# A feed-forward block's first stage: one width tile in full products in place of two, the next two in step, and four places for the last rows' inputs

## The chip, the cores and the metric

The kernel runs on one core of a Trainium2 chip. A core has a matmul engine (TensorE, in the profile PE, with its weight loads PEld), a vector engine (VectorE, DVE), an activation engine (ScalarE, ACT), a general engine (GpSimd, POOL) and a queue engine that issues most transfers (SyncE, SP). Each works through its own instructions in order; semaphores let one wait for another. Data lie in HBM, are brought into the on-chip SBUF by DMA, and matmuls write PSUM, which is in banks of 128 x 512 float32.

The metric is the device time of one execution in microseconds, as the median of several runs.

## What is computed

The reference is an encoder of two layers over 1024 tokens of width 1024. The token mixer is windowed attention in layer 0 and a gated linear recurrence in layer 1. Both layers end with the same kind of feed-forward block (ConvGLU), and it is this block that the change touches:

```python
def conv_ffn(v, w_in, conv_w, conv_b, w_out):
    gate, up = jnp.split(v @ w_in, 2, axis=-1)
    hid = jax.nn.gelu(dwconv_centred(gate, conv_w, conv_b)) * up
    return hid @ w_out

# of each layer, behind the mixer:
    f = conv_ffn(rmsnorm(h, norm_g[layer, 2]), ffn_w_in[layer], ffn_conv_w[layer],
                 ffn_conv_b[layer], ffn_w_out[layer])
    h = h + rmsnorm(f, norm_g[layer, 3])
```

`w_in` is 1024 x 5632, `w_out` 2816 x 1024, all in float32. The depthwise convolution runs along the tokens and is three wide.

## The kernel before

**Precision.** Every float32 operand of a matmul is split into a high part (a cast on ACT, line 88) and a low part (the difference, on DVE, line 89); a product is three matmuls, high by high, high by low and low by high (`mmk`, lines 531 to 538). Group names such as `wl<-st,wh` or `u7l<-c,u7h` are these low parts: `w` of weights, `u` of the activations. `uh` and `ul` hold the normalised activations of the block, transposed: 8 tiles of 128 of the width (k) by 1024 tokens. `ti` and `tj` are the two halves of the tokens, in layer 1 in the other order.

**The first stage** (`ffn`, from line 541; `first_units`, lines 680 to 741) makes gate and up for 22 tiles of 128 of the hidden width, one tile f after the other. A tile can be made in two ways:

- *In full* (`plain`, line 576): four PSUM groups, gate and up by ti and tj, each of 8 k-tiles by 3 matmuls, 96 matmuls of 128 x 512. It needs `uh` and `ul` as they are and two weight units made by `wunit`.
- *By block products* (`prod`, line 650): a Strassen-like scheme with seven products in place of eight, each of 4 k-tiles by 3 matmuls, so 84 matmuls. Product k multiplies a part of a weight unit (`operand`, line 645) with an operand B[k] made of the activations. B1, B2 and B3 are parts of `uh` and `ul` themselves; B4, B6 and B7 are made on DVE and ACT in tiles of their own, and B5 is written over the part of `uh` and `ul` with k 0 to 3 and tokens tj, so it can only be made when nobody needs that part any more. `operands` (line 597) makes them, in two halves of 128 x 1024 each.

The weight units of a tile in block products are four: a1 straight from HBM, the sums sx and sy, and a22. The sums are made by the DMA engines: `load` (line 622) issues plain loads of sx and sy on SP, and three accumulating transfers on POOL (line 632 into sx, lines 633 and 634 into the two halves of sy, each behind the one before it). a1 serves products 1 and 2, sx 5 and 7, sy 6 and 3, a22 product 4. `weights` (line 636) splits them into a ring of four places.

Before the change tiles 0 and 1 are made in full (`PLAIN = 2`). While PE works on them, DVE and ACT make the operands; after tile 1's full products B5 is split over its place. Tiles 2 to 21 follow in block products, in the order 2, 5, 6, 7, 3, then product 1 of the next tile, then 4. Behind each tile, `conv` (line 564) applies convolution, gelu and gating on ACT and DVE, and `hidden` (line 662) stores halves and their combinations in HBM for the second stage.

**The second stage** (lines 744 to 868) multiplies the hidden values with `w_out`, also in block products: seven sweeps over the 11 pairs of width tiles, in the order 1, 6, 7, 4, 2, 5, 3. Each step loads its two operands into the staging pool (`st`, four places; lines 753 and 754), splits them, and runs on four PSUM groups. `tail` (line 793) finishes a block of 128 tokens: it loads the block of the residual (`x<-h1d`, line 796), sums two squared norms (798), takes the power -0.5 on POOL (95), scales and adds (802) and stores (806). In layer 0 (`gnext`) it also normalises and transposes for the next layer (`norm_T`, lines 107 to 118). The blocks of the first half are finished in the middle of sweep 5, those of the second half behind sweep 3. There, at lines 846 to 855, DVE adds the PSUM group to a stored part (`y1`, 852), ACT squares and sums it (102), DVE multiplies it in place with the norm's weights (854), and `tail` follows. `x` has two places, so the load for a block waits until the store of the one two before it is done.

**What sets the order.** The program is written as a sequence of operations on tiles; a scheduler of the framework sets each engine's order from a model of the costs, and waits are put where a place in a pool or an operand isn't free. So the order on an engine isn't that of the text: DVE, for instance, makes operands in between the splits of weights. SP issues loads and stores in one order, and a load that waits for its place holds the ones behind it.

Of the kernel before, what the change touches and what calls it, by code (L numbers as in the profile page):

```python
# [6 lines left out]
F32 = mybir.dt.float32  # L7
# [4 lines left out]
ALU = mybir.AluOpType  # L12
# [4 lines left out]
P = 128  # L17
T = 1024
# [24 lines left out]

PLAIN = 2
# [4 lines left out]
def build(tc, A, out):  # L49
# [490 lines left out]
    def ffn(l, wo, dst, gnext, halves_, out_halves):  # L540
# [35 lines left out]
        def plain(f):  # L576

            wg = wo.first if f == 0 and wo.first else wunit(A["ffw1"][l, f, :, :1024])
# [3 lines left out]
            for (wh, wl), ps, m in ((wg, gi, ti), (wu, ui, ti), (wg, gj, tj), (wu, uj, tj)):  # L582
                mmk(ps, KT, lambda k: (wh[:, k * P:(k + 1) * P], wl[:, k * P:(k + 1) * P]),
                    lambda k: (uh[:, k, m], ul[:, k, m]), True)
# [5 lines left out]
            return conv(f, g, u)  # L590

        def operands():

            b12 = (uh[:, :4, tj], ul[:, :4, tj])
            late = []
            for kk in range(2):
                ks = slice(2 * kk, 2 * kk + 2)
                f32 = lambda x: x[:, ks].bitcast(F32)
                def tmp(t, b=1):
                    return fp.tile([P, 2, 512], F32, tag=t, bufs=b, name=t)  # L600
                def both(o, x, y, sub):
                    q = tmp("tt", 2)
                    dve.tensor_tensor(o, f32(x[0]), f32(y[0]), op=ALU.subtract)
                    dve.tensor_tensor(q, f32(x[1]), f32(y[1]), op=ALU.subtract)
                    dve.tensor_tensor(o, o, q, op=ALU.add)
                def more(o, a_, x, op):
                    dve.tensor_tensor(o, a_, f32(x[0]), op=op)
                    dve.tensor_tensor(o, o, f32(x[1]), op=op)
                x = tmp("c", 3)
                both(x, B[3], b12, True)  # L610
                split(B[7][0][:, ks], B[7][1][:, ks], x)
                more(x, x, B[1], ALU.add)
                nsplit(B[6][0][:, ks], B[6][1][:, ks], x)
                more(x, x, B[2], ALU.subtract)
                split(B[4][0][:, ks], B[4][1][:, ks], x)
                e1 = tmp("u") if kk else tmp("g")
                both(e1, B[1], b12, True)
                late.append((ks, e1))
            return late
# [60 lines left out]
        def first_units():  # L680
            for f in range(PLAIN):
                c = plain(f)
                if f == 0:
                    late = operands()
# [613 lines left out]
```

## Time and profile before

| | |
|---|---|
| runs of the kernel | 2732.56, 2733.25 and 2733.93 us, median 2733.25 |
| the profiled execution | 2730.61 us, of which its span 2728.8 us |
| granted clock, mean over the span | 0.993 |
| first stage of layer 0, first matmul to the second stage's first | 595.29 to 1023.67 us |
| first stage of layer 1 | 2079.45 to 2509.02 us |

The profile shows one execution. Times in it are in microseconds from the start of the span, unless marked ns. A row of an engine's timeline gives start, duration, engine, line, operation and what is written from what (`out<-in`), its shape and how many instructions of the kind follow each other; in square brackets stands how long the engine was idle before it, and what it waited for. A row of waits gives the waiting engine and line, what it waited for, the sum, the times and the longest. The chain of waits follows the end of the program back to what released each step. Consecutive instructions overlap, so that the distance of two starts is a little shorter than a duration.

### The profile page before, as it was taken

What the parts mean: (1) busy time and instruction counts of PE and PEld (TensorE: products, weight loads), DVE (VectorE), ACT (ScalarE), POOL (GpSimd) and SP (SyncE); (2) the same over time, 40 slices, a digit from 0 to 9 for tenths busy, and PEclk for the clock granted to TensorE, in tenths of its full rate; (3) what the DMA queues carried; (4) which work ended last, traced back from release to release, by engine and by line L of the source; (5) the groups of instructions that cost most, each with busy time, mean ns of one, the idle gap of its engine ahead of it and who ended that gap; (6) DMA issues with size and microseconds to landing.
All of it is one profiled execution on the core that took longest, in us unless ns stands there. A gap on an engine that the chain in (4) does not pass through costs nothing.

```text
span 2728.8 us, 37469 instructions
## 1 busy us (share of the span) xinstructions
PE 2660.9 (98%) x13496; PEld 2231.2 (82%) x13496; DVE 1828.1 (67%) x3034; ACT 1391.6 (51%) x2550; POOL 463.3 (17%) x514
## 2 busy tenths in 40 slices
PE   8999999999999999999999999999899999999998
PEld 7888887788888888887888888888788788888886
DVE  6588787678555565477686777868566856556446
ACT  6367667544444445454444545545454444444443
POOL 1231110211111100032232231312121111110013
PEclk9999999999999999999999999999999999999999
DMA  8683213656777857673234531111476687775666
GB/s 282 208 176 86 63 51 97 200 187 151 202 200 189 210 152 236 200 248 131 86 124 119 117 86 55 46 55 33 125 221 174 155 208 203 202 200 157 225 193 228
DMA packets 213579, 428.45 MB, mean 157 GB/s; under 512 B 20368, under 2 KB 77072, under 8 KB 207760
## 3 DMA queue, kind: packets, MB, share of 16 engines
q1 hardware_dynamic: 187264, 333.50, 38.0%
q0 software_dynamic: 23680, 88.09, 15.7%
q10 hardware_dynamic: 2448, 4.46, 0.5%
q8 instruction: 106, 1.74, 0.3%
q14 instruction: 81, 0.66, 0.1%
HBM read 333.17 MB, written 117.96 MB: 165 GB/s over the span
## 4 chain that ended last, share of the span: by engine, by line
PE 88%; DVE 7%; ACT 2%; DMA 1%; issue 1%; POOL 1%; SPq 0%; DVEq 0%; POOLq 0%; ACTq 0%
PE X L537 28%; PE V L537 11%; PE pj L83 7%; PE pj L84 7%; PE pj L85 7%; PE Y L537 5%; PE pb L83 3%; PE pb L84 3%; PE pb L85 3%; PE po L1118 1%; PE pa L1070 1%; PE pt L340 1%; PE pt L118 1%; PE pa L1050 1%; PE pu L1094 1%
## 5 line engine op out<-in xcount | busy, mean ns | idle before, releaser
L89 DVE TENSOR_TENSOR wl<-st,wh 128x1024 fp32r<-128x1024 f32 (+1 forms) x234 | 258.7, 1110 | 337.9 <-ACT wh L88 330.6
L88 ACT CAST wh<-st 128x1024 fp32r<-128x1024 f32 (+1 forms) x234 | 219.1, 938 | 291.3 <-PE X L537 180.9
L83 PE MATMUL pj<-uh,wh 128*128 128x512 f32 x512 | 206.3, 403 | 6.4 <-DVE xl L89 4.6
L537 PE MATMUL X<-wl,wh 128*128 128x512 f32 x528 | 205.7, 391 | 0.0
L537 PE MATMUL X<-wh,wl 128*128 128x512 f32 x528 | 205.5, 391 | 0.0
L84 PE MATMUL pj<-ul,wh 128*128 128x512 f32 x512 | 203.0, 397 | 0.1
L537 PE MATMUL X<-wh 128*128 128x512 f32 x528 | 201.0, 392 | 1.9 <-DVE c L846 1.9
L85 PE MATMUL pj<-uh,wl 128*128 128x512 f32 x512 | 202.9, 397 | 0.0
L83 PE MATMUL pj<-wh,uh 128*128 128x384 f32 (+1 forms) x512 | 190.8, 373 | 0.4 <-DVE v L282 0.4
L84 PE MATMUL pj<-wl,uh 128*128 128x384 f32 (+1 forms) x512 | 186.9, 365 | 0.0
L85 PE MATMUL pj<-wh,ul 128*128 128x384 f32 (+1 forms) x512 | 186.7, 365 | 0.0
L79 DVE TENSOR_TENSOR wl<-st,wh 128x1024 fp32r<-128x1024 f32 (+1 forms) x96 | 118.9, 1245 | 27.0 <-ACT wh L78 26.0
L537 PE MATMUL V<-uh,wh 128*128 128x512 f32 x344 | 133.9, 389 | 0.3 <-ACT uh L88 0.3
L537 PE MATMUL V<-ul,wh 128*128 128x512 f32 x344 | 134.0, 389 | 0.0
L537 PE MATMUL V<-uh,wl 128*128 128x512 f32 x344 | 133.9, 389 | 0.0
L78 ACT CAST wh<-st 128x1024 fp32r<-128x1024 f32 (+1 forms) x103 | 103.9, 1016 | 48.7 <-PE pj L84 27.2
L83 PEld LDWEIGHTS pj<-uh,wh 128*128 128x128 f32 x512 | 97.1, 190 | 26.7 <-DVE xl L89 5.5
L537 PEld LDWEIGHTS X<-wh 128*128 128x128 f32 x528 | 99.4, 188 | 23.8 <-issue 2.7
L1064 POOL TENSOR_TENSOR E<-EP,q 128x256 f32<-128x256 f32 x64 | 54.4, 850 | 371.3 <-DVE EP L1057 292.6
L537 PEld LDWEIGHTS X<-wl,wh 128*128 128x128 f32 x528 | 99.5, 189 | 21.0 <-DVE wl L89 0.5
L537 PEld LDWEIGHTS X<-wh,wl 128*128 128x128 f32 x528 | 99.5, 189 | 21.0
L85 PEld LDWEIGHTS pj<-uh,wl 128*128 128x128 f32 x512 | 97.2, 190 | 19.6
(337 smaller groups left out, 7322.1 us busy)
## 6 DMA issues: line engine op xcount, KB each, us to landing
st<-hid SPq DMA_DIRECT2D x154, 256.0 KB, 3.2
st<-in_ffw_dram SPq DMA_DIRECT2D x106, 256.0 KB, 3.2
w2s<-in_ffw_dram POOLq DMA_DIRECT2D x24, 1024.0 KB, 8.0
st<-in_ffw_dram SPq DMA_DIRECT2D x48, 512.0 KB, 3.6
hid<-tt SPq DMA_DIRECT2D x88, 256.0 KB, 4.6
st<-w2s SPq DMA_DIRECT2D x88, 256.0 KB, 3.4
sx<-in_ffw_dram SPq DMA_DIRECT2D x80, 256.0 KB, 3.9
sy<-in_ffw_dram SPq DMA_DIRECT2D x40, 512.0 KB, 5.8
```

What stands on the lines that cost most here:

```text
L78: act.copy(h[:, :n], raw)
L79: (eng or dve).tensor_tensor(l[:, :n], raw, h[:, :n].bitcast(F32), op=ALU.subtract)
L83: pe.matmul(o, ah, bh, start=first, stop=False)
L84: pe.matmul(o, ah, bl, start=False, stop=False)
L85: pe.matmul(o, al, bh, start=False, stop=last)
L88: act.copy(h, src)
L89: dve.tensor_tensor(l, src, h.bitcast(F32), op=ALU.subtract)
L118: pe.transpose(ps[:, k, :], u[:, (4 * b + k) * P:(4 * b + k + 1) * P], ident)
L340: pe.transpose(tp[:, j, :], sm[:, j, c * P:(c + 1) * P], ident)
L537: pe.matmul(o, x, y, start=new, stop=e, skip_group_check=not first)
L1050: pe.matmul(pa[:, c, :], E2[:, cs], E1[:, cs], start=True, stop=True)
L1064: pool.tensor_tensor(gl, pl_, ql, op=ALU.mult)
```

## The change

In the first stage of both layers only tile 0 is made in full, and its two tj groups run k 0 to 3 first, then k 4 to 7. Tiles 1 and 2 are made in block products side by side, one product for both and then the next: 1 and 2 (which need only the activations of ti), 5, 3, 6, 7, 4. `operands` is now a generator that makes B5, then B6, B7 and B4, each from the one before by an addition or subtraction, and the program text calls it between the products. As a second tile is open, its up and gate values lie in places of the scratch pool `tt`, its product 5 in the place of `s1`. Tile 3's loads and splits begin during product 7, its products 2 and 1 (the first of the sequence from there) around product 4 of tiles 1 and 2. The store of the hidden values of tiles 0, 1 and 2 follows after that.

In the second stage, `rows` loads the residual's blocks ahead of `tail`. The four blocks of the second half are loaded together when the last sweep's matmuls are issued; in layer 0 they have four places in their own pool, in layer 1 they use the staging pool's. The product with the norm's weights goes to a tile of its own, `y2`, which no longer overwrites what ACT reads.

In the diff the body of the old `operands`, which the kernel's text above shows, is cut.

```diff
@@ -40,8 +40,6 @@
 
 LAST = (6, 10)
 HOLD = (4, 7)
-
-PLAIN = 2
 
 AHEAD = 2000
 
@@ -575,48 +573,61 @@
 
         def plain(f):
 
-            wg = wo.first if f == 0 and wo.first else wunit(A["ffw1"][l, f, :, :1024])
+            wg = wo.first if wo.first else wunit(A["ffw1"][l, f, :, :1024])
             wu = wunit(A["ffw1"][l, f, :, 1024:])
             bank = lambda t: psx.tile([P, 512], F32, tag=t, name=t)
             gi, ui, gj, uj = bank("X"), bank("Y"), bank("V"), bank("Y")
-            for (wh, wl), ps, m in ((wg, gi, ti), (wu, ui, ti), (wg, gj, tj), (wu, uj, tj)):
-                mmk(ps, KT, lambda k: (wh[:, k * P:(k + 1) * P], wl[:, k * P:(k + 1) * P]),
-                    lambda k: (uh[:, k, m], ul[:, k, m]), True)
+            def some(w, ps, ks, m, first):
+                wh, wl = w
+                mmk(ps, len(ks), lambda k: (wh[:, ks[k] * P:(ks[k] + 1) * P], wl[:, ks[k] * P:(ks[k] + 1) * P]),
+                    lambda k: (uh[:, ks[k], m], ul[:, ks[k], m]), first)
+            some(wg, gi, range(KT), ti, True)
+            some(wu, ui, range(KT), ti, True)
+
+            for ks in (range(4), range(4, KT)):
+                some(wg, gj, ks, tj, ks[0] == 0)
+                some(wu, uj, ks, tj, ks[0] == 0)
+            yield
             g = gtile()
             u = fp.tile([P, T], F32, tag="u", bufs=1, name="u")
             for gp, up_, m in ((gi, ui, ti), (gj, uj, tj)):
                 act.activation(g[:, m], gp, AF.Copy, scale=-1.0)
                 act.copy(u[:, m], up_)
-            return conv(f, g, u)
+            yield conv(f, g, u)
 
         def operands():
 
...
-            return late
+            xs = [fp.tile([P, 2, 512], F32, tag="c", bufs=3, name="c") for _ in range(2)]
+            tmp = lambda: fp.tile([P, 2, 512], F32, tag="tt", bufs=2, name="tt")
+            half = lambda x, kk: x[:, 2 * kk:2 * kk + 2]
+            def more(o, x, part, kk, op):
+                for c in range(2):
+                    dve.tensor_tensor(o, x, half(part[c], kk).bitcast(F32), op=op)
+                    x = o
+            def out_of(sp, k, kk, x):
+                sp(half(B[k][0], kk), half(B[k][1], kk), x)
+            for kk, x in enumerate(xs):
+                q = tmp()
+                f32 = lambda t, c: half(t[c], kk).bitcast(F32)
+                dve.tensor_tensor(x, f32(B[1], 0), f32(B[5], 0), op=ALU.subtract)
+                dve.tensor_tensor(q, f32(B[1], 1), f32(B[5], 1), op=ALU.subtract)
+                dve.tensor_tensor(x, x, q, op=ALU.add)
+            for kk, x in enumerate(xs):
+                out_of(split, 5, kk, x)
+            yield
+            for kk, x in enumerate(xs):
+                more(x, x, B[3], kk, ALU.add)
+                out_of(nsplit, 6, kk, x)
+            yield
+            for kk, x in enumerate(xs):
+                q = tmp()
+                more(q, x, B[1], kk, ALU.subtract)
+                out_of(split, 7, kk, q)
+            yield
+            for kk, x in enumerate(xs):
+                more(x, x, B[2], kk, ALU.subtract)
+                out_of(split, 4, kk, x)
+            yield
 
         def load(f):
 
@@ -678,29 +689,75 @@
                 nc.sync.dma_start(hd[k, p], x)
 
         def first_units():
-            for f in range(PLAIN):
-                c = plain(f)
-                if f == 0:
-                    late = operands()
-                hidden(f, c)
-                if f == PLAIN - 1:
-                    for ks, e1 in late:
-                        split(B[5][0][:, ks], B[5][1][:, ks], e1)
-            raws = {f: load(f) for f in (PLAIN, PLAIN + 1)}
-            gen = weights(raws.pop(PLAIN))
-            ops = list(gen)
-            X = [psx.tile([P, 512], F32, tag="X", name="X")]
-            s = {}
+            X, s, ops = [], {}, []
+
+            def xbank():
+                X.append(psx.tile([P, 512], F32, tag="X", name="X"))
 
             def start(units):
 
+                xbank()
                 prod(1, operand(units, 1), X[-1], True)
                 s[1] = fp.tile([P, 512], F32, tag="s1", bufs=1, name="s1")
                 act.copy(s[1], X[-1])
 
+
+            tiles = (1, 2)
+            pl, opd = plain(0), operands()
+            next(pl)
+            raws = {f: load(f) for f in tiles}
+            gens = {f: weights(raws.pop(f)) for f in tiles}
+            us = {f: [next(gens[f])] for f in tiles}
+            more_of = lambda: [us[f].append(next(gens[f])) for f in tiles]
+            next(opd)
+            c0 = next(pl)
+            next(opd)
+            us_, gs, vs, s5 = {}, {}, {}, {}
+            for f in tiles:
+                start(us[f])
+                y = psx.tile([P, 512], F32, tag="Y", name="Y")
+                prod(2, operand(us[f], 2), y, True)
+                us_[f] = fp.tile([P, T], F32, tag="u" if f == 1 else "tt", bufs=1 if f == 1 else 2, name="u")
+                dve.tensor_tensor(us_[f][:, ti], y, s[1], op=ALU.add)
+            more_of()
+            for f in tiles:
+                vs[f] = psx.tile([P, 512], F32, tag="V", name="V")
+                prod(5, operand(us[f], 5), vs[f], True)
+                s5[f] = fp.tile([P, 512], F32, tag="s5" if f == 1 else "s1", bufs=1, name="s5")
+                act.copy(s5[f], vs[f])
+            more_of()
+            next(opd)
+            for f in tiles:
+                prod(3, operand(us[f], 3), vs[f], False)
+            for f, x in zip(tiles, X):
+                prod(6, operand(us[f], 6), x, False)
+                su = fp.tile([P, 512], F32, tag="su", bufs=1, name="su")
+                act.copy(su, x)
+                dve.tensor_tensor(us_[f][:, tj], vs[f], su, op=ALU.add)
+            more_of()
+            next(opd)
+            raws[3] = load(3)
+            gen = weights(raws.pop(3))
+            for f, x in zip(tiles, X):
+                prod(7, operand(us[f], 7), x, False)
+                gs[f] = gtile() if f == 1 else fp.tile([P, T], F32, tag="tt", bufs=2, name="tt")
+                act.copy(gs[f][:, tj], x)
+                dve.tensor_tensor(gs[f][:, tj], gs[f][:, tj], s5[f], op=ALU.add)
+                ops.append(next(gen))
+            cs = {}
+            for f, x in zip(tiles, X):
+                prod(4, operand(us[f], 4), x, False)
+                act.copy(gs[f][:, ti], x)
+                ops.append(next(gen))
+                cs[f] = conv(f, gs[f], us_[f])
+            raws[4] = load(4)
+            hidden(0, c0)
+            for f in tiles:
+                hidden(f, cs[f])
+            del X[:]
             start(ops)
             yield
-            for f in range(PLAIN, NF):
+            for f in range(3, NF):
                 if f + 2 < NF:
                     raws[f + 2] = load(f + 2)
                 gen = weights(raws.pop(f + 1)) if f + 1 < NF else None
@@ -732,7 +789,6 @@
                 dve.tensor_tensor(u[:, tj], v, su, op=ALU.add)
                 ahead()
                 if f + 1 < NF:
-                    X.append(psx.tile([P, 512], F32, tag="X", name="X"))
                     start(nxt)
                 prod(4, w(4), x, False)
                 act.copy(g[:, ti], x)
@@ -789,11 +845,18 @@
         Xs, Vs = left(), [psr.tile([P, 512], F32, tag="v", name="V") for _ in range(4)]
         tok = lambda b, t: slice((4 * b + t) * P, (4 * b + t + 1) * P)
 
-        def tail(b, t, ya, sa, yb, sb):
+        def rows(b, t):
+
+            if gnext or b == ia:
+                x = np_.tile([P, D], F32, tag="x", bufs=4 if gnext else 2, name="x")
+            else:
+                x = stg.tile([P, D], F32, tag="st", name="st")
+            nc.sync.dma_start(x, h1d[l][tok(b, t), :])
+            return x
+
+        def tail(b, t, ya, sa, yb, sb, x):
 
             ts_ = tok(b, t)
-            x = np_.tile([P, D], F32, tag="x", bufs=2, name="x")
-            nc.sync.dma_start(x, h1d[l][ts_, :])
             sq = np_.tile([P, 1], F32, tag="sq", name="sq")
             dve.tensor_tensor(sq, sa, sb, op=ALU.add)
             rs = rstd_of(np_, sq, 1, D, "p")
@@ -837,7 +900,9 @@
                     mms(k, p, h, l_, ps, range(4), k in (1, 5, 2) and p == 0)
                 if k == 5 and p in (1, 3, 5, 7):
                     t = p // 2
-                    tail(ia, t, y["c11"][:, t, :], ss["q11"][:, t:t + 1], y["c21"][:, t, :], ss["q21"][:, t:t + 1])
+                    tail(ia, t, y["c11"][:, t, :], ss["q11"][:, t:t + 1], y["c21"][:, t, :], ss["q21"][:, t:t + 1], rows(ia, t))
+            if k == 3:
+                last = [rows(ib, t) for t in range(4)]
             for t in range(4):
                 if k in (1, 6, 7, 4):
                     act.copy(y[{1: "c11", 6: "c12", 7: "c22", 4: "c21"}[k]][:, t, :], ps[t])
@@ -847,12 +912,13 @@
                 else:
                     for p, h, l_ in hold:
                         mms(k, p, h, l_, ps, (t,), False)
-                    sb = np_.tile([P, 1], F32, tag="sb", name="sb")
+                    sb = np_.tile([P, 1], F32, tag="sb", bufs=1, name="sb")
                     y1 = np_.tile([P, 512], F32, tag="y1", name="y1")
                     dve.tensor_tensor(y1, ps[t], y["c12"][:, t, :], op=ALU.add)
                     sumsq(np_, y1, sb)
-                    dve.tensor_tensor(y1, y1, g3[:, D0], op=ALU.mult)
-                    tail(ib, t, y1, sb, y["c22"][:, t, :], ss["q22"][:, t:t + 1])
+                    y2 = np_.tile([P, 512], F32, tag="y2", bufs=1, name="y2")
+                    dve.tensor_tensor(y2, y1, g3[:, D0], op=ALU.mult)
+                    tail(ib, t, y2, sb, y["c22"][:, t, :], ss["q22"][:, t:t + 1], last[t])
             if k == 4:
                 scaled("c21", "q21", D1)
             elif k == 5:
```

25 lines of the change are left out of this document (removed).

## The prediction

> **What bounds the kernel now.** I read the busy table of the page first, then its chain that ended last, and then stretches around the two feed-forward stages that the diff touches.
>
> ```profile
> span 2728.8 us, 37469 instructions
> PE 2660.9 (98%) x13496; PEld 2231.2 (82%) x13496; DVE 1828.1 (67%) x3034; ACT 1391.6 (51%) x2550; POOL 463.3 (17%) x514
> PE 88%; DVE 7%; ACT 2%; DMA 1%; issue 1%; POOL 1%; SPq 0%; DVEq 0%; POOLq 0%; ACTq 0%
> ```
>
> The matmul engine is busy 98% of the span and carries 88% of the chain. So two things are worth time: matmuls that disappear, and the few places where PE waits. Everything on DVE, ACT, POOL or a queue costs only where PE ends up behind it. The next view is busy time per window (us; then busy and count of PE, PEld, DVE, ACT, POOL; granted clock, DMA share, GB/s): the first stage of each feed-forward block from its first matmul to that of the second stage, the start of the first one, and a steady stretch.
>
> ```profile
> 595.29:1023.67 428.38, 426.54 (x1884) 352.05 (x1883) 267.29 (x287) 192.11 (x247) 53.09 (x62) 1.00 0.70 185
> 2079.45:2509.02 429.57, 426.51 (x1884) 351.98 (x1882) 268.78 (x288) 193.50 (x248) 53.10 (x62) 1.00 0.71 185
> 631.29:643.29 12.00, 11.98 (x53) 9.57 (x51) 12.00 (x12) 3.78 (x5) 1.61 (x2) 1.00 0.51 134
> ```
>
> The clock is full, and DVE, idle a third of the span, has no gap at all from 631.29 to 643.29, where the operands are made. The chain of waits gives the price of a matmul, and the list of PE's waits the stalls near the start (layer 0: 590 to 680, layer 1: 2074 to 2165) and at each first stage's end.
>
> ```profile
> 2254.99 5.44 PE X L537 x24
> PE X L537 <- ACT s L699: 0.4, 1, 0.4
> ...
> PE X L537 <- DVE u6l L561: 1.0, 1, 1.0
> ...
> PE V L537 <- ACT uh L88: 0.3, 1, 0.3
> ...
> PE X L537 <- ACT g L728: 1.4, 1, 1.4
> ```
>
> 24 matmuls take 5.44 us: 0.2267 each. The wait for s occurs in both layers, u6l and uh only in layer 1. A stage has 2×96 + 20×84 = 1872 of them, 424.4 us; its 12 small instructions are about 0.9 us (eight transposes are 0.87, below). What is left is 3.1 us in layer 0 and 4.3 in layer 1. Taking out 1.4 for the wait for g and some 0.2 to fill the pipe again, the start costs about **1.5 us** in layer 0 and **2.7 us** in layer 1.
>
> **The change part by part.**
>
> *Matmuls removed.* Tile 1 goes from 96 to 84 in both layers: 24 × 0.2267 = **−5.44 us**. This part is certain; the rest is what it costs at the start.
>
> *Operands.* B5 must now be written over uh and ul before any product can use it, so tile 0 runs k 0–3 of both its tj groups first. By the new order PE does 24 + 24 + 12 + 24 = 84 matmuls and eight transposes before k 4–7.
>
> ```profile
> 595.29 0.48 PE L537 MATMUL X<-uh,xwh 128*128 128x512 f32 x1
> 606.82 0.87 PE pt L118 x8
> 627.43 1.22 DVE L607 TENSOR_TENSOR c<-c,uh 128x1024 f32<-128x1024 f32 x1
> 628.57 1.22 DVE L603 TENSOR_TENSOR g<-uh 128x1024 f32<-128x1024 f32 x1
> 663.17 0.68 DVE L675 TENSOR_TENSOR tt<-tt,c 128x512 f32<-128x512 f32 x1
> 663.77 0.68 DVE L89 TENSOR_TENSOR wl<-st,wh 128x512 fp32r<-128x512 f32 x1
> 649.19 1.05 ACT L88 CAST u4h<-c 128x1024 fp32r<-128x1024 f32 x1 [0.20 <-DVE c L608]
> ```
>
> So k 0–3 is done at 595.29 + 84 × 0.2267 + 0.87 = 615.2; a cast (1.05) and two low parts later, with what lies between them, B5 stands at about 618.9. One row starts 1.14 us after the one before when full size, 0.60 when half. In the new DVE order 29 instructions run from there to the second half of u7l: 23 large and 6 small, 26.2 + 3.6 = 29.8 us; with 0.9 for the wait of tile 2's first add (tile 1's partial result has to be read before its place is free) it is ready at 649.6. PE gets there after 228 matmuls: 595.29 + 51.7 + 0.9 = 647.9, and about 648.7 with gaps of the kind it has now. That is a wait of about 1 us. The second: tile 3's first weight unit takes the place of one that tile 1's product 7 still reads. Its cast and low part (1.05 + 1.2) follow that read, and PE, which has 5 to 6 matmuls of tile 2 left, waits about 0.7 us. Either wait adds some 0.2 to fill the pipe. All other operands come by this count before their matmuls (B6's second half 3 us early). Layer 1 has the same order from its own start: 1.3 and 0.65. I take 2.1 us of start stalls in layer 0 (before 1.5) and 2.3 in layer 1 (before 2.7): together **+0.2 us**. Bounds: all start stalls gone, −4.2; each of the four waits 2.5 longer, +10. I lean to the middle as DVE's work for operands falls (26 large instructions where there were 28 per layer) but now has to be done by product 7.
>
> Of what moves with it: conv and hidden of tiles 1 and 2 come after product 4, behind DVE's operand work, where the steady stretch has DVE slack; SP and POOL get one more load of a tile per layer (six DMAs on SP less two weight loads, three on POOL), beside a DMA share of 0.5. Cost 0; without that cover tile 4's units would be late, a few us.
>
> *Sums of weights.* Three accumulating DMAs on POOL make a tile's sx and sy. They now feed tile 1, not tile 2.
>
> ```profile
> 615.92 0.87 POOL L633 DMA_DIRECT2D sy<-sx  x1 [3.46 <-DMA sx<-in_ffw_dram]
> 619.91 0.86 POOL L633 DMA_DIRECT2D sy<-sx  x1 [3.13 <-DMA sx<-in_ffw_dram]
> 620.84 0.86 POOL L634 DMA_DIRECT2D sy<-sy  x1
> 623.66 0.86 POOL L634 DMA_DIRECT2D sy<-sy  x1 [1.96 <-DMA sy<-sx]
> 2104.08 0.86 POOL L634 DMA_DIRECT2D sy<-sy  x1 [0.17 <-issue]
> 2107.09 0.86 POOL L634 DMA_DIRECT2D sy<-sy  x1 [2.15 <-DMA sy<-sx]
> sy<-sy POOLq DMA_DIRECT2D x40, 256.0 KB, 5.5
> 654.75 1.05 ACT L88 CAST wh<-sx 128x1024 fp32r<-128x1024 f32 x1 [0.24 <-PE V L537]
> 658.38 1.05 ACT L88 CAST wh<-sy 128x1024 fp32r<-128x1024 f32 x1
> ```
>
> The second tile's sums are cast at 654.75 and 658.38 now, some 30 us after they land. With 5.5 to landing, the sy of the two tiles are there at 626.3 and 629.2 in layer 0 and 2109.6 and 2112.6 in layer 1; sx at 615.9 and 619.9 at the latest. DVE reaches their low parts, by its new order, at 620.0 and 625.7 (sx), 629.2 and 632.6 (sy), in layer 1 at 2113.4 and 2116.8 (sy). Less a cast and a hand-over (1.2), 1.7 to 4.6 us are in hand. Cost 0, bounds 0 and one us per us beyond that margin, since everything on DVE up to u7l stands behind it.
>
> DVE is full with instructions of two inputs while POOL issues these sums, and the gaps between dependent issues are 2 to 3.5 us all the same. [...]
>
> *Rows of layer 0's end.* PE waits once for DVE, which stands in order behind work that waited for x.
>
> ```profile
> PE X L537 <- DVE c L846: 1.9, 1, 1.9
> 1193.57 1.42 DVE L802 SCALAR_TENSOR_TENSOR x<-c,prs,x 128x512 f32<-128x512 f32 x2 [0.56 <-DMA x<-h1d]
> 1204.85 1.28 DVE L114 SCALAR_TENSOR_TENSOR nu<-x,nrs,g 128x1024 f32<-128x1024 f32 x1 [0.73 <-POOL nrs L95]
> 1207.19 0.68 DVE L846 TENSOR_TENSOR c<-X,c 128x512 f32<-128x512 f32 x1
> ```
>
> With four places the loads no longer wait behind stores in SP's queue, and the new DVE order has this c ahead of the fourth nu, so one 1.28 us instruction leaves the way: 1.9 becomes about 0.7, **−1.2 us**. Bounds 0 (another low part takes its place) and −3 (the wait gone, and the next layer's start up to 1 earlier).
>
> *The kernel's end.* Here the profile shows DVE waiting for x, then for ACT.
>
> ```profile
> 2713.25 2.59 DMA out_dram<-x
> 2715.84 0.02 issue
> 2715.85 3.50 DMA x<-h1d
> 2719.28 0.40 PE L537 MATMUL X<-wh,wl 128*128 128x512 f32 x1
> 2719.48 0.75 DVE L802 SCALAR_TENSOR_TENSOR x<-y,prs,x 128x512 f32<-128x512 f32 x1 [2.53 <-DMA x<-h1d]
> 2720.81 0.68 DVE L852 TENSOR_TENSOR y<-X,c 128x512 f32<-128x512 f32 x1
> 2722.34 0.69 DVE L854 TENSOR_TENSOR y<-y,g 128x512 f32<-128x512 f32 x1 [0.85 <-ACT junk L102]
> 2722.95 0.15 DVE L798 TENSOR_TENSOR sq<-sb,q 128x1 f32<-128x1 f32 x1
> ```
>
> The load of x waits for the store of an earlier row to free its place. With the four loads early, the last y starts when the last matmul is done, 2719.28 + 0.40 and a hand-over, 2719.72 in place of 2720.81: −1.1. With y2 a tile of its own, L854 no longer stands between ACT's sum of squares and L798: −0.6 of its time. I take **−1.6 us**; bounds −1.0 and −1.9. The places ("st") that the loads borrow come free with the last units' low parts, some 10 us ahead.
>
> *Sum:* −5.4 + 0.2 − 1.2 − 1.6 = **−8.0 us**. The profiled execution took 2730.61 us (its span 2728.8), 2.64 under the median of the three runs, 2733.25. On the median this gives **2725.2**.
>
> **The rivals.** (a) *DVE keeps ahead.* If PE's own gaps put it at product 7 a microsecond later, the waits vanish: −8.0 − 4.4 = −12.4, about 2721. For it speaks that PE is never as fast as a count; against it that DVE has no gap in the third window row.
>
> (b) *The change's gain is eaten.* DVE's 29 instructions are a chain in order, and each one late by 1.14 is late for PE too. Three us more per layer, less than three large instructions, give −8.0 + 6 = −2: about 2731. The wait for u6l in layer 1 is this very mechanism, now at 1.0. The same time comes out if the early rows save nothing because other loads take their place in SP's queue, and the stalls are 1.5 longer per layer.
>
> (c) *Slower: the sums come late.* If accumulating DMAs on POOL, now wanted at once, land L us later than counted, PE waits L minus the margin of 1.7 in layer 0 and 2.6 in layer 1. Over 0.2% slower means +5.5, so 13.5 us must be lost: it decides from L = 8.9 on, and L = 10 gives −8.0 + 15.7 = +7.7, about 2741. That is a landing after 15 us where the row has 5.5. For it: the second sums follow a chain of three transfers, and DMAs are denser then. Against: the six POOL rows, alike in both layers.
>
> That the change doesn't do what it says I count under (b): the matmul count is in the program, only the loads could fail to be early.
>
> **How the numbers follow.** Forecast 0.48, (a) 0.14, (b) 0.26, (c) 0.12. A measurement of this kernel tells about 0.2%, 5.5 us, from no change: faster is below 2727.8, slower above 2738.7. The forecast (own range 2722 to 2727.8) and (a) are faster, 0.62; (b) is the same, 0.26; (c) slower, 0.12. The range leaves out the far part of (a), beyond the sum of the low ends, and most of (c): 2719 to 2737.
>
> **What would show it.** First stages with 1872 instructions of PE in place of 1884, about 426.3 us (layer 0: 428.38 − 2.72 + 0.6) and 426.4 (layer 1: 429.57 − 2.72 − 0.4). PE's waits near 50 us into each: one for u7l, about 1, and one for the low part of tile 3's first unit, about 0.7; more, or a wait for sx or sy's low part, shows (b) or (c). DVE's wait for x gone at 2719, PE's wait for c at 0.7 or less, and DVE's last two y adds 1.1 us earlier behind the last matmul. It is wrong if the stages do not shrink, with PE's waits saying behind what.

## The result

| | median, us | runs, us |
|---|---|---|
| before | 2733.59 | 2731.71 to 2736.41 (6) |
| changed | 2721.28 | 2716.81 to 2726.44 (6) |

The ratio is 0.9959, 95% interval 0.9949 to 0.9970: 12.3 us by the medians, 8.2 to 13.9 us by the interval. A second series gave 2719.08 beside 2732.05, ratio 0.9955 (0.9943 to 0.9968). The forecast was 8.0 us. The direction is right; the size is just short of the interval, and the terms of the sum were not all the ones that made it. The two profiled executions lie 9.9 us apart, not 12.3: that of before is 3.0 us under its median, that of the changed kernel 0.6. The parts below account for the 9.9; no profile shows the rest.

The changed kernel's page, its busy table and chain:

```profile
span 2718.9 us, 37473 instructions
PE 2656.1 (98%) x13472; PEld 2228.1 (82%) x13472; DVE 1830.8 (67%) x3040; ACT 1396.6 (51%) x2556; POOL 472.8 (17%) x520
PE 89%; DVE 6%; ACT 2%; DMA 2%; issue 1%; SPq 0%; POOL 0%; DVEq 0%; POOLq 0%; ACTq 0%
```

PE's count fell by 24 (13496 to 13472), its busy time by 4.8 us; the span fell by 9.9. So about half of the difference is time in which PE was not busy (matmuls at half clock, below, count as busy). Where it came from shows when both traces are cut at the same events. The first stages, in the view of windows, from the first matmul to the second stage's first:

```profile
597.35:1023.44 426.09, 423.91 (x1871) 349.71 (x1870) 269.02 (x287) 195.72 (x251) 55.83 (x65) 1.00 0.73 190
2074.30:2501.57 427.27, 423.70 (x1871) 349.62 (x1870) 270.68 (x291) 195.84 (x253) 55.85 (x65) 1.00 0.73 191
```

They were 428.38 and 429.57. All parts of the span, before and after, in us (each worked out as a difference of two such events):

| part | before | after | difference | forecast |
|---|---|---|---|---|
| start to layer 0's first stage | 595.29 | 597.35 | +2.06 | 0 |
| first stage, layer 0 | 428.38 | 426.09 | −2.29 | −2.1 |
| second stage of layer 0, and layer 1's mixer up to PE's wait for xl (near 1842) | 821.21 | 818.33 | −2.88 | −1.2 |
| from there to layer 1's first stage (end of the mixer, its output projection) | 234.57 | 232.53 | −2.04 | 0 |
| first stage, layer 1 | 429.57 | 427.27 | −2.30 | −3.1 |
| second stage of layer 1 to the end | 219.78 | 217.33 | −2.45 | −1.6 |

The sum is −9.9, as the spans say. The first line is chance: no edit acts there, and over the 13 profiles of this study (eleven programs, two of them taken twice) that part lies between 593.84 and 597.95 us whatever the kernel; the changed kernel alone has 597.35 and 593.84. By chance, too, it is as large as the −2.04 in layer 1's projection, which nobody forecast.

PE's waits in the changed kernel near the starts (560 to 700; 1930 to 2160), then at layer 0's second stage (990 to 1060) and at its end (1170 to 1300):

```profile
PE Y L535 <- DVE wl L87: 0.5, 1, 0.5
PE X L535 <- DVE u7l L87: 0.3, 1, 0.3
...
PE X L535 <- DVE u7l L87: 1.7, 1, 1.7
...
PE Y L535 <- DVE wl L87: 0.5, 1, 0.5
...
PE X L535 <- ACT g L785: 1.4, 1, 1.4
PE X L535 <- ACT c L908: 1.3, 1, 1.3
...
PE pa L1116 <- DVE E L1113: 0.3, 1, 0.3
PE pj L81 <- DVE s L1038: 0.3, 1, 0.3
PE pt L116 <- DVE ul L87: 0.3, 1, 0.3
```

The two waits that the forecast named at the start, for u7l and for the low part of tile 3's first unit (the one written Y ... wl), are there, and those of before (for s, u6l and uh) are gone. At layer 0's end the wait of 1.9 for c is gone; in its place stands one of 1.3 (1.25) near 1055, far from anything the prediction looked at: c L908 is the copy of the second stage's first sums.

**Half clock.** What the prediction did not see at all is what a PE wait of about 2 us can do to the matmuls behind it (when it does and when not stands in the last section). Before, right after the wait of 1.94, in PE's timeline and the granted clock (the third column from the end of a window row, 0.51):

```profile
1208.02 0.70 PE L537 MATMUL X<-wh 128*128 128x512 f32 x1 [1.94 <-DVE c L846]
1208.52 0.63 PE L537 MATMUL X<-wl,wh 128*128 128x512 f32 x1
1208.94 0.63 PE L537 MATMUL X<-wh,wl 128*128 128x512 f32 x1
...
1208.00:1211.50 3.50, 3.48 (x8) 2.73 (x9) 3.50 (x6) 3.15 (x7) 1.72 (x2) 0.51 0.90 315
```

Starts 0.43 us apart in place of 0.23, for eight matmuls: 1.67 us more, nearly as much as the wait itself. The same stretch of the changed kernel:

```profile
1208.00:1211.50 3.50, 3.50 (x17) 2.90 (x16) 3.50 (x4) 1.93 (x3) 0.18 (x1) 1.00 0.73 236
```

Seventeen matmuls in the time of eight. So layer 0's end gave 1.94 + 0.2 (filling the pipe) + 1.67, and another 1.0 with a wait for a transposed row near 1253 (0.73 and its filling), 4.8 in all; the new wait took 1.4 of it back, and other small ones about 0.4. That makes the −2.9 of the table.

The end of the kernel, PE's last row and then DVE's timeline of the changed one:

```profile
2711.36 0.39 PE L535 MATMUL X<-wh,wl 128*128 128x512 f32 x1
2711.79 0.69 DVE L917 TENSOR_TENSOR y<-X,c 128x512 f32<-128x512 f32 x1 [2.83 <-PE X L535]
2712.52 0.69 DVE L920 TENSOR_TENSOR y<-y,g 128x512 f32<-128x512 f32 x1
2713.33 0.16 DVE L861 TENSOR_TENSOR sq<-sb,q 128x1 f32<-128x1 f32 x1
2714.40 0.75 DVE L865 SCALAR_TENSOR_TENSOR st<-y,prs,st 128x512 f32<-128x512 f32 x1 [0.72 <-POOL prs L93]
```

The last y starts 0.43 us behind the last matmul's start (before 1.53), sq 1.54 behind y (before 2.14): −1.10 and −0.60, to the hundredth what was forecast. DVE now waits for PE at this place, for x no more. The last transfers were 0.3 shorter, and PE's way to the last matmul 0.5. These 0.5 are not the change's to keep: a second profile of the changed kernel has the same end behind the last matmul, but PE's way there is 1.3 longer, with waits of 0.8 for c and 0.2 for a weight's low part near 2681 and 2693.

### The profile page after: what moved, and what is told of

It reads as the page before. It is cut to its first block, busy times and chain, and to the rows that moved or that the text cites. A ratio compares the mean times of both kernels' runs of the same rounds, so it can differ in the third digit from the quotient of the medians.

```text
span 2718.9 us, 37473 instructions
## 1 busy us (share of the span) xinstructions
PE 2656.1 (98%) x13472; PEld 2228.1 (82%) x13472; DVE 1830.8 (67%) x3040; ACT 1396.6 (51%) x2556; POOL 472.8 (17%) x520
## 4 chain that ended last, share of the span: by engine, by line
PE 89%; DVE 6%; ACT 2%; DMA 2%; issue 1%; SPq 0%; POOL 0%; DVEq 0%; POOLq 0%; ACTq 0%
PE X L535 29%; PE V L535 11%; PE pj L81 8%; PE pj L82 7%; PE pj L83 7%; PE Y L535 5%; PE pb L81 3%; PE pb L82 3%; PE pb L83 3%; PE po L1184 1%; PE pa L1136 1%; PE pt L116 1%; PE pt L338 1%; PE pa L1116 1%; PE pu L1160 1%
```

## The experiments

Two theories stood at first. **A**: the parts of the change act where they stand and add up. **B**: the gain is the first stage's, and what the second stages showed is a shift in when the half clock strikes. "Before" in each series is the old kernel on the same chip, 2732.14 in the first (21 runs).

**First stage alone**, with the old tail: `rows`, `last` and `y2` taken out.

```diff
-        def rows(b, t):
...
-                    tail(ib, t, y2, sb, y["c22"][:, t, :], ss["q22"][:, t:t + 1], last[t])
+                    dve.tensor_tensor(y1, y1, g3[:, D0], op=ALU.mult)
+                    tail(ib, t, y1, sb, y["c22"][:, t, :], ss["q22"][:, t:t + 1])
```

> The change's first stage with the tail of before (two places for the residual's rows, loads inside tail, y1 multiplied in place). Theory A (the parts of the change act where they stand, and add up): the two first stages are 2.3 us shorter each, as in the changed kernel (layer 0: 423.7 to 421.5 from the first matmul to the wait for g; layer 1: 427.0 to 424.8), the end is 9.5 us from the last matmul's start as in before, and layer 0's second stage shows a PE wait of about 2 us behind DVE again, with about eight matmuls at half clock (1.6 us) after it; time about 2728.5. Rival B (most of the gain comes from the first stage, and what the second stages showed was a shift in the phase of the clock gate): the wait of 2 us may be there, but the time is 2724 or less.

Measured: 2726.40, ratio 0.9978 (0.9970 to 0.9987), between the two. Its stages and its waits in layer 0's second half (1024 to 1300):

```profile
597.66:1023.75 426.09, 423.91 (x1872) 349.72 (x1870) 268.95 (x287) 195.72 (x251) 55.80 (x65) 1.00 0.73 190
2075.30:2502.34 427.04, 423.56 (x1871) 349.71 (x1870) 271.30 (x291) 196.18 (x253) 55.87 (x65) 1.00 0.73 191
...
PE pt L116 <- DVE ul L87: 1.4, 2, 1.1
PE X L535 <- DVE c L902: 1.1, 1, 1.1
PE X L535 <- DVE wl L87: 0.6, 1, 0.6
```

The first stages are those of the changed kernel to 0.3 us. (The expectation's 423.7 and 421.5 for layer 0 do not fit the traces: from the first matmul to the one behind the wait for g it is 425.5 before and 423.2 here.) The wait for c is back at layer 0's end, but with 1.1 (1.15) and without half clock, and the end is 8.9 us from the last matmul's start, not 9.5: two misses of A. So with the old tail, too, layer 0's second part is 1.1 shorter than before (820.15). And the output projection of layer 1, where no edit acts, is 231.41 us, shorter still than in the changed kernel.

**Tail alone**, with the first stage of before (the reverse diff).

> The first stage of before (two tiles in full) with the change's tail: rows ahead, four places, y2. Theory A: no PE wait for the second stage's last c in layer 0 and no half clock behind it, so 3 to 4 us there, and 2 us at the end (7.5 us from the last matmul's start): about 2727.5. Rival B: only the end's 2 us, about 2731.5.

Measured: 2727.51, ratio 0.9985 (0.9976 to 0.9994); A's time. The stages are the old ones:

```profile
597.95:1026.32 428.37, 426.53 (x1883) 352.06 (x1882) 267.27 (x287) 192.11 (x247) 53.09 (x62) 1.00 0.70 185
2079.09:2508.68 429.59, 426.53 (x1883) 352.09 (x1882) 268.78 (x288) 193.51 (x248) 53.10 (x62) 1.00 0.70 185
```

Layer 0's second part is 818.33, as in the changed kernel, with its new wait near 1055 (1.31); the end 1.7 us shorter than before; the part with the output projection 234.44, as before. So 0.22% and 0.15% of the two halves make the 0.41% of the whole within their intervals: in the time, A holds. Place by place it does not quite: in layer 0's second part the halves give −1.1 and −2.9, and both together −2.9. And the −2 us of layer 1's projection belong to the first stage's edit, though they stand elsewhere: in all eleven profiles with a new first stage this part takes 231.4 to 233.1, in the two with the old one 234.4 and 234.6.

**Without y2**:

```diff
-                    y2 = np_.tile([P, 512], F32, tag="y2", bufs=1, name="y2")
-                    dve.tensor_tensor(y2, y1, g3[:, D0], op=ALU.mult)
+                    dve.tensor_tensor(y1, y1, g3[:, D0], op=ALU.mult)
```

> The changed kernel, with the multiplication by the norm's weights written over y1 again (no y2). Theory A: DVE's L920 waits for ACT's sum of squares, and the end from the last matmul's start grows by 0.6 us (7.5 to 8.1); nothing else of note: about 2722. Rival: the wait on ACT also stands in DVE's order in layer 0's second stage and brings a PE wait back there, with half clock: 3 us and more, 2725.

Measured: 2721.97, ratio 0.9965 (0.9952 to 0.9977). From the last matmul's start to the end 8.16 us where the changed kernel has 7.54: the 0.6 of the forecast. The rest of A's expectation failed: layer 0's second part took 822.26, 3.9 longer. Not at its end, but at the new wait near 1055, here 2.33 with eight matmuls at half clock, and 1.7 in a wait of PE for E later. The first is not y2's doing: the changed kernel itself had 2.6 there in its second profile (below). Whether the second is, no run shows.

**Rows late again**, y2 kept: each load at the call of `tail`, two places, no `last`.

> The changed kernel with the rows' loads inside tail and two places again, y2 kept. Theory A: the last block waits for its row again, 1.1 us at the end (7.5 to 8.6), and the PE wait of about 2 us with half clock behind it comes back in layer 0: about 2726. Rival (the loads were hidden anyway, the gain at both places was y2's or the order's): under 1 us, about 2722.

Measured: 2722.65, ratio 0.9968 (0.9956 to 0.9981). The time is the rival's (2722), not A's (2726), but the end does grow, and by 2.45 (7.54 to 9.99) in place of 1.1, for two rows wait one after the other, as DVE's timeline has it:

```profile
2712.76 0.75 DVE L862 SCALAR_TENSOR_TENSOR x<-y,prs,x 128x512 f32<-128x512 f32 x1 [3.56 <-DMA x<-h1d]
...
2718.32 0.75 DVE L862 SCALAR_TENSOR_TENSOR x<-y,prs,x 128x512 f32<-128x512 f32 x1 [2.35 <-DMA x<-h1d]
```

At layer 0's end the wait for c is 1.27, without half clock, so A missed there; and the new wait near 1055 is gone. Layer 0's second part takes 818.87, where the changed kernel has 818.33 in one profile and 821.45 in another: in layer 0 the early rows gained next to nothing on balance, since what they save at its end they cost near 1055. That puts the question: does the change itself make that wait? SP's timeline, changed kernel first, then this one:

```profile
1038.90 1.19 SPq L854 DMA_DIRECT2D x<-h1d  x2
1040.25 0.67 SPq L809 DMA_DIRECT2D st<-w2s  x1
1040.97 0.60 SPq L810 DMA_DIRECT2D st<-hid  x1
1044.05 1.51 SPq L854 DMA_DIRECT2D x<-h1d  x2
1045.99 0.32 SPq L809 DMA_DIRECT2D st<-w2s  x1
```

```profile
1038.87 1.13 SPq L851 DMA_DIRECT2D x<-h1d  x2
1040.23 0.55 SPq L809 DMA_DIRECT2D st<-w2s  x1
1042.42 0.32 SPq L810 DMA_DIRECT2D st<-hid  x1
```

With four places free, all four rows of the first half are issued as soon as the pool exists, some 140 us before they are used. The second pair stands in SP's queue ahead of the second stage's units; these come later, ACT waits for one in order, the copies L908 stand behind it on ACT, and PE waits for their PSUM. ACT's timeline in the second profile of the changed kernel names the transfer:

```profile
1051.49 0.63 ACT L558 ACTIVATE wh<-st 128x512 fp32r<-128x512 f32 x1 [3.92 <-DMA st<-w2s]
1052.03 1.06 ACT L908 COPY c<-X 128x512 f32<-128x512 f32 x2
```

**Two and two places**: the same four places, but two (`x`) for the first half's four rows and the second half's first two, two more (`xl`) for the second half's last two, and the second half's loads kept in program order.

```diff
-                x = np_.tile([P, D], F32, tag="x", bufs=4 if gnext else 2, name="x")
+                x = np_.tile([P, D], F32, tag="x" if b == ia or t < 2 else "xl", bufs=2, name="x")
...
-            nc.sync.dma_start(x, h1d[l][tok(b, t), :])
+            i = nc.sync.dma_start(x, h1d[l][tok(b, t), :])
+            if gnext and b == ib:
+                tc.keep_in_program_order(i)
```

> The changed kernel with the four places of layer 0 parted: two for the first half's rows, two more for the second half's, whose loads are kept in program order. Theory (the PE wait of 1.25 us for c near 1055 us, new with the change, comes from the two more rows that SP now loads there, ahead of the second stage's units): the wait is gone, layer 0's second stage 1.4 us shorter (385.9 to 384.5) as long as its end stays without a wait of 2 us: about 2720. Rival (that wait is from the change of the first stage or from another order on ACT): it stays at 1.2.

Measured: 2722.35, ratio 0.9969 (0.9958 to 0.9981). The wait near 1055 is gone. With all profiles its cause is shown: in the six profiles whose program issues four rows there, PE waits there for 0.5 to 2.6 us, in the seven others not at all. But the first half's third and fourth row now wait again for the stores of the first two (issued at 1185.4 and 1188.3), DVE comes to them 6 to 8 us later in the stage than in the changed kernel, and layer 0's part takes 822.21. Its largest wait, for c at 1204, stands ahead of the second half's loads (from 1216.8 on), so these can't have caused it, and behind the late rows on DVE, as before; how the others came about was not tried (waits from 1021 to 1300):

```profile
PE X L535 <- DVE c L913: 1.7, 1, 1.7
PE pa L1118 <- DVE E L1115: 1.2, 1, 1.2
PE pt L116 <- DVE ul L87: 1.0, 1, 1.0
```

**One tile alone**: tile 1 in block products while operands are made, tile 2 as every later one. The matmul count is the changed kernel's.

```diff
-            tiles = (1, 2)
+            tiles = (1,)
...
-            for f in range(3, NF):
+            for f in range(2, NF):
```

> The changed kernel with tile 1 alone in block products while operands are made, tile 2 following as every later tile (same number of matmuls). Theory (side by side, the two tiles buy time for DVE's chain: product 7 starts 60 matmuls, 13.6 us, later): alone, PE reaches product 6 some 5 us and product 7 some 11 us before the operand; the first stages are 8 to 12 us longer each, with waits for u6l, u7l, u4l, and half clock behind some: about 2742. Rival (the operands are early enough anyway): within 2 us of the changed kernel.

Measured: 2720.86, ratio 0.9964 (0.9951 to 0.9978); far from my 2742, and within 2 us of the changed kernel, as the rival has it. But its stages:

```profile
594.53:1022.79 428.26, 424.56 (x1871) 349.70 (x1870) 270.81 (x291) 196.68 (x252) 55.67 (x65) 1.00 0.72 190
2072.21:2500.31 428.10, 424.34 (x1871) 349.51 (x1870) 270.10 (x289) 196.64 (x252) 55.68 (x65) 1.00 0.72 190
```

In layer 0 that is the time of before (428.38): what 12 matmuls gave went into waits, for low parts of weights and for su. Side by side is worth 2.2 us in layer 0 and 0.8 in layer 1, in these two stages; the time of the whole does not show it. It isn't worth 10, since the scheduler by itself draws tile 2's first products between tile 1's, as the program's order of PE shows.

**B4 behind B7**: the remaining wait for u7l. In the changed kernel's DVE timeline, layer 1, four large instructions of B4 (three additions into c, and u4l) stand ahead of u7l's second half:

```profile
2117.67 1.22 DVE L605 TENSOR_TENSOR c<-c,uh 128x1024 f32<-128x1024 f32 x1
...
2120.01 1.22 DVE L605 TENSOR_TENSOR c<-c,ul 128x1024 f32<-128x1024 f32 x1
...
2123.48 1.22 DVE L87 TENSOR_TENSOR u4l<-c,u4h 128x1024 fp32r<-128x1024 f32 x1
...
2125.75 1.23 DVE L605 TENSOR_TENSOR c<-c,uh 128x1024 f32<-128x1024 f32 x1
...
2128.09 1.22 DVE L87 TENSOR_TENSOR u7l<-tt,u7h 128x1024 fp32r<-128x1024 f32 x1
```

```diff
-                    dve.tensor_tensor(o, x, half(part[c], kk).bitcast(F32), op=op)
+                    i = dve.tensor_tensor(o, x, half(part[c], kk).bitcast(F32), op=op)
+                    if pin and c == 0:
+                        tc.keep_in_program_order(i)
...
-                more(x, x, B[2], kk, ALU.subtract)
+                more(x, x, B[2], kk, ALU.subtract, pin=True)
```

(and the generator's call for B4 stands right behind that for B7)

> The changed kernel with DVE made to finish B7's low parts before it begins B4's additions (pinned in program order). Theory (the remaining stall at the start is DVE's chain of operands in order): u7l's second half is four large instructions, 4 to 5 us, earlier; PE's wait for u7l (0.3 in layer 0, 1.7 in layer 1) goes, and no wait for u4l comes in its place, as PE reaches product 4 some 5 us after product 7: first stages 422.9 and 422.5 (from 423.2 and 424.4). Rival (DVE has no slack, the wait moves to u4l or to the low parts of tile 3): 423.2 and 424.4 or longer, with such a wait in the list.

Measured: 2718.31, ratio 0.9954 (0.9941 to 0.9966). Layer 1's stage is 1.2 us shorter (427.27 to 426.05), layer 0's the same (426.12). Up to the wait for g, as the expectation counts, that is 423.2 and 423.3: the theory's way in layer 1, though by 1.2 and not 1.9, and the rival's in layer 0. u7l is no longer waited for; u4l is, by 0.2, in both layers. u7l's second half came 1.8 us earlier in the stage, not 4 to 5: where B4's instructions had stood, DVE now waits 1.12 and 1.21 us for casts on ACT. So the new order helps, but what then holds DVE up at this place is ACT. **Both together** (with two and two places):

> B4 behind B7 and the parted places together. By theory the sum of both: 2 to 2.5 and 1.4 us less than the changed kernel, about 2718. Rivals as for the single ones: no better than the changed kernel, 2721.

Measured: 2725.00, ratio 0.9971 (0.9962 to 0.9980), not the sum of both that theory had (2718): the short layer 1 (426.07) and the long layer 0 part (822.50) add up.

**B4 behind B7 and paced rows**: four places, the first half's third and fourth row loaded shortly before their use, the second half's early.

```diff
+                if gnext and k == 5 and p == 1:
+                    late = {t: rows(ia, t) for t in (2, 3)}
```

(these two loads pinned in program order; in the trace all four rows of the first half are then issued at 1165, some 16 to 22 us before DVE reads them)

> The changed kernel with B4 pinned behind B7, and in layer 0 the third and fourth row of the first half loaded just before they are needed (sweep 5's second step), so that SP issues them no longer at the second stage's start, while the second half's rows stay early. Theory (the wait for c near 1055 is the price of loading rows there, the wait for c near 1207 the price of loading the last rows late; both can be had): no wait above 0.5 at either place, no half clock behind them, and layer 0's part from the wait for g to hgrn's wait for xl at 820 or less (821.2 in the changed kernel): about 2717. Rival (the two are exclusive, rows loaded at any time displace units): a wait of 1 us or more at one of the two places, 2719 or more.

Measured: 2719.25, ratio 0.9950 (0.9936 to 0.9963), layer 0's part 816.81 (819.7 from the wait for g, as the expectation counts), and no wait of PE above 0.3 between 1030 and 1300: the stage is the theory's, the time nearer to the rival's 2719. A last pair on one chip:

> The changed kernel once more, beside the next one on the same chip: 2721 us. Its stages from the wait of 0.97 on are the same to 0.1 us as in its first profile (423.2, 385.9, 424.4), and any difference of the whole time stands ahead of the first feed-forward stage or behind a PE wait of 2 us.

> The version with B4 behind B7 and paced rows, beside the changed kernel on the same chip. Theory: the 2.7 us by which its stages are shorter show in the median, about 2718.5. Rival (what the waits gave is lost again near the end, where its profile was 1 us longer): within 1 us of the changed kernel.

Measured: 2719.08 for the changed kernel, 2717.62 for this version, ratio 0.9947 (0.9933 to 0.9960). The difference of 1.5 us lies between the theory's 2.7 and the rival's 1, and the intervals overlap, so the time alone doesn't part them; the stages do: 816.98 (816.81 in its first profile) where the changed kernel has 821.45 here and 818.33 in its first profile, and 426.02 for 427.29. The changed kernel's expectation failed at the end (1.3 longer, with no wait of 2 us, as said above) and in one stage: its wait near 1055 was 2.6 this time, with half clock (waits from 1021 to 1100; window 1054 to 1057):

```profile
PE X L535 <- ACT c L908: 2.6, 1, 2.6
...
1054.00:1057.00 3.00, 3.00 (x8) 2.34 (x7) 1.62 (x3) 1.61 (x4) 0.00 (x0) 0.50 0.57 173
```

In that profile layer 0's part gained nothing against before (821.45 and 821.21): the new wait ate all that layer 0's end gave.

## Why the prediction was right, and where it was not

- **Matmuls and start**: forecast −5.4 + 0.2, measured −4.6. The count is right. The two waits are those named: 0.3 and 0.5 in layer 0 (forecast 1.0 and 0.7), 1.7 and 0.5 in layer 1 (1.3 and 0.65). Taking off the later start of 2.06, u7l's low part begins at 647.9 and ends 1.2 later, forecast ready at 649.6: the chain of 29 instructions was counted well. What was mis-sized is the cost of the start before: of my 1.5 and 2.7 us only the part with named waits (0.4 and 1.7) went away, and the rest, about 1 us a layer, stayed beside the new waits.
- **"With four places the loads no longer wait behind stores in SP's queue"** is the step that failed, by half. It is true at layer 0's end, and I didn't ask what else free places set off: loads that are issued at once, in front of others. Price in the changed kernel: 1.4 us in one profile, about 4.4 (2.6, its filling and the half clock) in the other.
- **Layer 0's end** was forecast at −1.2. It gave −4.8, since the wait went wholly, a second one with it, and the half clock behind it, of which the prediction knew nothing although both stood in the trace of before. That early rows take the wait away, as the forecast had it, the runs show: PE does not wait for c there in the eight profiles in which the first half's third and fourth row come early, and for 1.15 to 1.94 in the five others. But only the 1.94 had half clock behind it: beside the new first stage the rows are worth 1.2 to 1.7 there (1.15 with the first stage's edit alone, 1.27 with rows late again, 1.6 and 1.7 with two and two places), not 3.8.
- **Layer 1's projection**: 0 forecast, −2.0 measured, and shown to be the first stage's doing by the two halves of the change. Before has two waits for oh of 1.59 and 1.50 with matmuls at half clock behind, the tail alone has 1.46 and 1.50 without; after has 0.40 and 1.49. The order of one store and of a few transposes differs there; that this is the cause was not tried.
- **The end**: −1.6 forecast, −1.7 by the two named steps, −2.45 with what lies around, of which 0.5 did not come again in the second profile. Rows late again cost 2.45, as two rows wait in a row, where the forecast had one.
- **Rivals.** (c) didn't happen: in the changed kernel no wait of PE near either start is for a sum, and the second tiles' sy were issued at 622.0 (POOL) and cast at 632.84. But the margin was smaller than counted: in layer 1 ACT waits 2.72 us for tile 1's sy (cast at 2104.28), and DVE makes the low part right behind the cast. And one reading against (c) was wrong: DVE was not full while POOL issued the sums of before, but idle for 5.49 us up to 620.50, across the first two rows. The changed kernel shows what those rows could not: from 2095.92 to 2103.19 DVE is busy all the time, and the four issues there follow each other by 1.3 to 2.7 us. (b) didn't happen with two tiles; it is what one tile alone does in layer 0. (a)'s time, 2721, is the one that came, though not by its mechanism: the waits at the start stayed.
- **Luck.** The number came out as near as it did in part by chance: in the place of layer 0's −1.2 stands −2.9, the balance of −4.8, +1.4 and about +0.4; layer 1's projection, −2.0, had no term at all; and in the profiles the start's chance +2.1 hides as much.

## What to carry to other kernels

Removing matmuls from a bound engine is worth their number only if the operands for the rest keep pace; work out the chain on the engine that makes them, in its own order (a second tile's worth of cover gave 2.2 and 0.8 us in the two stages here). More places for a load are also permission to load early: look at what the queue then issues in front of others, and pace it. A wait of 2 us on the matmul engine is to be priced at up to twice its length, as the 1.94 here with 3.8 in all.

## What the runs showed of the hardware

In 13 profiles, PE's waits of 1.2 to 1.75 us among large matmuls (26 for g, all 1.4; 13 for q, 1.36; six for u7l, six for c) never had slow matmuls behind them; waits of the mixer that stand among small matmuls or close together are left out here. Those of 2.14 to 2.25 us near 1842 had them in 7 of 13 cases, those of 2.49 near 327 in 13 of 13, and the three of 1.94, 2.33 and 2.64 in layer 0's second stage each. Of those left out, near 492, a wait of 1.89 and one of 2.21 had them, eleven of 1.82 to 2.06 did not. So the length alone does not decide.

What does shows in the granted clock. In each profile the stretches at half clock are 3.41 us long, or a few times that, and all lie on one grid of 3.41 us (the last one runs out with the kernel). The wait near 1842 cut at this grid, the slot with the wait and the one behind it, first in the changed kernel, then in the second profile of B4 behind B7 with paced rows (PE's busy time stands behind the comma):

```profile
1839.06:1842.47 3.41, 1.26 (x6) 0.76 (x5) 3.41 (x11) 2.69 (x8) 0.00 (x0) 1.00 0.00 0
1842.47:1845.89 3.42, 3.42 (x10) 2.64 (x9) 3.42 (x9) 1.26 (x5) 1.52 (x2) 0.50 0.02 5
...
1835.55:1838.96 3.41, 1.69 (x7) 1.43 (x8) 3.41 (x10) 2.42 (x8) 0.78 (x1) 1.00 0.02 5
1838.96:1842.38 3.42, 3.42 (x18) 2.88 (x17) 3.42 (x11) 0.88 (x4) 0.76 (x1) 1.00 0.00 0
```

The first wait, 2.15 us, lies in one slot whole, and the next slot runs at half the clock. The second, 2.25 us, is the longer one, but a grid line cuts it, 1.72 us are left in the slot, and nothing follows. From 320 us on, without the small matmuls of attention (400 to 430), 37 slots of the 13 profiles hold 1.89 us of waiting or more, and the slot behind each of them is at half clock; behind a slot at full clock with 1.78 us or less that happened once (1.75, before, near 1949). So a wait of about 2 us is worth some 1.6 us more or nothing, by how it falls on the grid. The scatter of a kernel's runs, 5 to 10 us here, may be made of such draws; that was not tried by itself. The Trainium skill, TensorE: Matmul & The Clock Gate, section "Part 1: The HAM clock gate (the "warmup" mystery)", says that the clock is gated by a free-running window of about 3.4 us: half rate after an idle window, full rate after a busy one. The grid and the 3.41 us at half clock agree with it; that a wait of 1.89 us in one slot suffices, in the middle of dense work, does not follow from a window that must be idle throughout.
